# One hybrid SSD, gMLP and expert layer on one core: d_skip as rows, v and half of w_o in 512 columns, a shorter gelu

## The chip, the cores and the metric

The kernel runs on one core of a Trainium2 chip. The metric is the device time of one execution in microseconds (us). The engines are called PE (matmuls), DVE (VectorE), ACT (ScalarE), POOL (GpSimd) and SP, which here only issues loads. 16 DMA engines serve all queues of the core.

## What is computed

One layer of a backbone over 512 latent tokens and 256 context tokens with 1024 channels, cut to what the change touches:

```python
xm_l = rmsnorm(h, norm1_w) * (1 + sc1_l) + sh1_l      # sc, sh, g: slices of silu(c) @ ada_w + ada_b
p_l = xm_l @ w_in                                     # 512 x 7200
y_l, xh_l = ssd_scan_bidir(p_l[..., :N_SCAN], ...)    # conv, chunked scan in both directions
y = y + d_skip[:, None] * xh                          # 16 heads
g = rmsnorm_by_group(y * silu(z))                     # ssd branch
u, v = split(gelu(uv))                                # uv: 2048 columns of p_l
v = layernorm(v); sgu = u * (w_s mixes v over 128 positions + b_s)
merged = sigmoid(gate_a) * (ssd @ w_pa) + sigmoid(gate_b) * (sgu @ w_pb)
h = h + g1_l * (merged @ w_o)
h = h + g2_l * expert_choice_ffn(rmsnorm(h, norm2_w) * (1 + sc2_l) + sh2_l)   # 16 experts, 64 tokens each
return rmsnorm(h, final_norm_w)
```

## The kernel before

Everything is fp32. A product of two fp32 matrices is taken as three matmuls on halves: each operand is split into a high part (`wh`, a cast on ACT, L73) and a low part (`wl`, a subtraction on DVE, L74), and PE adds high × high, low × high and high × low in one accumulator. The helper `wsplit` does this for weights with high priority. Weight tiles of 1 MB come from a pool of two (`wtile`), loaded by SP.

The work in order of time. First SP loads x (L96, four loads) and the modulation weights `aw` (L193, two loads of 512 KB), then slices of `w_in` and the context tokens `ct` (L206). POOL issues small loads of its own in this time: the rows of the vectors (L88), `alog` (L124, one row of 32 numbers to all 128 partitions), `dtb` (L127) and the skip weights `dsk` (L130, two loads). PE begins with a matrix by vector product, `aux<-aw,scp` at L237, whose result is the first slice of the modulation; then it transposes the normalised x (L255) and the context (L261), and the first projection follows. The skip weights are read in the scan, at L527.

Then come convolution and scan by groups. v follows, through the helper `token_major` (L583): for each of four blocks of 256 columns and each half of the eight 128-row blocks of weights, 4 token tiles × 4 row blocks × 3 matmuls (L601 to L603), 96 instructions for a pair of halves. When a block's second half is through for a token tile, `evac` is called; for v it is `v_out`, which takes `gelu2` (L608 to L614: square on ACT, three DVE operations around a tanh on ACT) and after every second block the statistics for the layer norm (L623). While v runs, `steps(scans, 2)` puts pieces of the scan between its chunks. After the last block, L636 normalises v, and only then the tile that `w_s` is loaded into becomes free (L751); PE transposes `w_s` (L760) and mixes v. The u stage and the other projections use `cols` (L714 for the loads, L358 to L360 for the matmuls, 512 columns each); u calls `gelu2` as well, on 512 columns.

At the end of the mixer `token_major` runs again with `w_o` and `residual` (L915 to L921): multiply with the gate on DVE into the scratch `t0`, add x on DVE, square with a sum on ACT back into `t0`, which has one buffer. Between the chunks the router is prepared, and `logits(nb)` (L926 to L948) transposes finished columns and multiplies them with the router weights. Then come the choice of tokens, the eight pairs of experts with their weights in 1 MB pieces (L673, `fetch`), and the output.

The instructions are placed by a scheduler that follows the program order, priorities and free buffers, so the order on an engine changes with the code.

Of the kernel before, what the change touches and what calls it, by code (L numbers as in the profile page):

```python
# [20 lines left out]
NT = 4  # L21
# [12 lines left out]
def tile_backbone(  # L34
# [10 lines left out]
    def dram(t, off, ap):  # L45
        return bass.AP(tensor=t.tensor, offset=t.offset + off, ap=ap)

    def row_bc(t, off=0, n=1024):
        return dram(t, off, [[0, 128], [1, n]])
# [19 lines left out]
    def wtile():  # L69
        return wp.tile([128, 2048], F32, name="w")  # L70
# [5 lines left out]
    def wsplit(hi, lo, src, lo_eng=None):  # L76
        with tc.high_priority():
            split(hi, lo, src, lo_eng)
# [47 lines left out]
    G.memset(dtb, 0.0)  # L126
    nc.gpsimd.dma_start(dtb[0:32, :], dram(dt_bias, 0, [[1, 32], [1, 1]]))  # L127
    dsk = sp.tile([128, NK], F32, bufs=1)
    for s in range(2):
        nc.gpsimd.dma_start(dsk[64 * s:64 * s + 64, :], dram(d_skip, s, [[0, 64], [2, NK]]))  # L130

    def rsqrt(o, v, scr, n):

# [30 lines left out]
    def acc():  # L164
        return ps.tile([128, 512], F32, name="acc")
# [186 lines left out]
    def hl_tile(a, b):  # L352
        return [hl.tile([128, 1024], F32R, name=n)[:, :a * b].rearrange("p (a b) -> p a b", a=a) for n in ("wh", "wl")]
# [8 lines left out]
    def w_cols(src, c0, n):  # L362
        return dram(src, c0, [[src.shape[1], 128], [128 * src.shape[1], NK], [1, n]])
# [194 lines left out]
    def ahead(gen):  # L558

        cur = next(gen)  # L560
        for n in gen:
            yield cur
            cur = n
        yield cur
# [15 lines left out]
            scans = ssd_group(g)  # L580


    def token_major(src, n0, lh, ll, evac, wt=lambda nb: wtile()):  # L583

        def weights():
            for nb in range(4):
                w = wt(nb).rearrange("p (k n) -> p k n", k=NK)
                load(w, w_cols(src, n0 + 256 * nb, 256))
                for kh in range(2):
                    wh, wl = hl_tile(4, 256)  # L590
                    wsplit(wh, wl, w[:, 4 * kh:4 * kh + 4, :])
                    yield nb, kh, wh, wl

        for nb, kh, wh, wl in ahead(weights()):
            if kh == 0:
                pp = [acc()[:, :256] for _ in range(NT)]
            for t in range(NT):
                for k in range(4):
                    kt = 4 * kh + k
                    a = slice(128 * t, 128 * t + 128)  # L600
                    T.matmul(pp[t], lh[:, kt, a], wh[:, k, :], start=kt == 0, stop=False)  # L601
                    T.matmul(pp[t], ll[:, kt, a], wh[:, k, :], start=False, stop=False)  # L602
                    T.matmul(pp[t], lh[:, kt, a], wl[:, k, :], start=False, stop=kt == NK - 1)  # L603
                if kh == 1:
                    evac(nb, t, pp[t])
            yield

    def gelu2(o, p, a):  # L608

        S.activation(a, p, AF.Square)  # L610
        V.tensor_scalar(a, a, GELU_C * GELU_K, GELU_C, op0=OP.mult, op1=OP.add)
        V.tensor_mul(a, a, p)
        S.activation(o, a, AF.Tanh)
        V.scalar_tensor_tensor(o, o, 1.0, p, op0=OP.add, op1=OP.mult)  # L614

    vt = big.tile([128, NT, 1024], F32, name="F")
    bn = sp.tile([128, NT, 2, 6], F32, bufs=1)

    def v_out(nb, t, p):
        a = sp.tile([128, 512], F32, name="tm")[:, :256]  # L620
        gelu2(vt[:, t, 256 * nb:256 * nb + 256], p, a)
        if nb % 2:
            V.bn_stats(bn[:, t, nb // 2, :], vt[:, t, 256 * nb - 256:256 * nb + 256])  # L623

    for _ in token_major(W, 4128, xmh, xml, v_out):
        steps(scans, 2)
    steps(scans, 99)
    mv = sp.tile([128, NT, 2], F32, bufs=1)
# [51 lines left out]
    def fetch(n):  # L680
        while len(queue) < n:
            w = next(pieces, None)
            if w is None:
                return
            queue.append(w)
# [187 lines left out]
    def half(name, n=512):  # L873
        return rp.tile([128, 512], F32, name=name)[:, :n]
# [17 lines left out]
    def router_weights():  # L892

        p = aux()
        T.transpose(p[:, 0:32], mrow, ident[:32, :32])
        V.tensor_copy(mcol, p[:, 0:32])
        V.scalar_tensor_tensor(mcol[:, 8:16], mcol[:, 8:16], 1.0, mcol[:, 16:24], op0=OP.add, op1=OP.mult)
# [15 lines left out]
    h = big.tile([128, NT, 1024], F32, name="F")  # L913
    ssq = rp.tile([128, NT, 4], F32, bufs=1)

    def residual(nb, t, p):
        cs = slice(256 * nb, 256 * nb + 256)
        a = half("t0", 256)
        V.tensor_mul(a, p, g1b[:, cs])
        V.tensor_add(h[:, t, cs], a, x2[:, t, cs])  # L920
        S.activation(a, h[:, t, cs], AF.Square, accum_out=ssq[:, t, nb:nb + 1])  # L921

    pl, pt = aux(), aux()

    def logits(nb):

        at = full("m1").rearrange("p (k n) -> p k n", k=2)
        for k in (2 * nb, 2 * nb + 1):
            p = aux()
            for t in range(NT):  # L930
                T.transpose(p[:, 128 * t:128 * t + 128], h[:, t, 128 * k:128 * k + 128], ident)
            if k == NK - 1:
                V.tensor_copy(at[:, k % 2, :], p)
            else:
                S.copy(at[:, k % 2, :], p)
        for k in (2 * nb, 2 * nb + 1):
            if nb == 3:
                for t in range(NT):
                    T.matmul(pt[:, 16 * t:16 * t + 16], at[:, k % 2, 128 * t:128 * t + 128], rwl[:, k % 2, :],
                             start=False, stop=k == NK - 1, skip_group_check=True)  # L940
            else:
                g = slice(32 * (k % 4), 32 * (k % 4) + 32)
                T.matmul(pl[g, :], rw[:, k, :], at[:, k % 2, :], start=nb < 2, stop=k in (2, 3, 4, 5))
        if nb == 2:
            a = half("t0")
            S.copy(a, pl)
            for t in range(NT):
                T.matmul(pt[:, 16 * t:16 * t + 16], a[:, 128 * t:128 * t + 128], sel32[:, 0:16],  # L948
                         start=t == 0, stop=False, skip_group_check=True)

    for i, _ in enumerate(token_major(w_o.rearrange("l k n -> (l k) n"), 0, mgh, mgl, residual)):
        if i in {0:11}:
            fetch({0:11}[i])
        if i == 0:
            router_weights()
        elif i == 1:
            router_shift()
            V.tensor_copy(rwl, rw[:, 6:8, 0:16])
            before = half("t1").bitcast(BF)[:, :896]
            steps_ = half("t0").bitcast(I16)[:, :896]  # L960
            G.iota(steps_, pattern=[[1, 896]], base=-384, channel_multiplier=-1)
            V.tensor_scalar(before, steps_, 0.0, -2.0 ** -60, op0=OP.is_le, op1=OP.mult)
        elif i % 2 == 0:
            logits(i // 2 - 1)
    logits(3)
    es_xm.close()
    es_hl.close()
    es_mid.close()
# [160 lines left out]
    for pr in range(NE // 2):  # L1129
# [38 lines left out]
        def evac(name, c0, c1, pd):  # L1168
            a = half(name, c1 - c0)
            V.scalar_tensor_tensor(a, pd, gi[:, 0:1], g2k[:, c0:c1], op0=OP.mult, op1=OP.mult)  # L1170
            return a
# [99 lines left out]
```

## Time and profile before

| | us |
|---|---|
| median of the three times shown | 1179.45 |
| the other two | 1177.4 and 5647.97 (the first) |
| the profiled execution | 1177.17 |
| its span | 1175.4 |

The span runs from the first to the last instruction in the trace; 1.8 us of the profiled execution's time lie around it. Times in rows are counted from the start of the span. The stages, by the trace: loads and first modulation until about 26 us, first projection, convolution and scan until 237, v until 297.5, u and the other projections until 584, w_o until 646, routing until 661, the experts to the end. The mean granted clock of PE is 0.99 of 2.4 GHz.

### The profile page before, as it was taken

The numbers are of one execution on the slowest core, as the hardware profiler recorded it, in microseconds if no ns is written. First come the engines' busy times: TensorE is split into PE (matmuls) and PEld (weight loads), VectorE is DVE, ScalarE is ACT, GpSimd is POOL, SyncE is SP. The second block draws the span as 40 slices with busy tenths as digits, with TensorE's granted clock in tenths as the row PEclk, the third lists the DMA queues.
The fourth block names the chain that finished last, engine by engine and source line by source line (L and its number), as shares of the span: only waits on it lengthen the run. The fifth ranks groups of instructions, "written<-read, shape, count | busy, mean of one in ns | idle before, by whom it ended". The sixth has DMA issues, their size and how long they took to land.

```text
span 1175.4 us, 15016 instructions
## 1 busy us (share of the span) xinstructions
PE 1081.8 (92%) x5939; PEld 711.1 (61%) x5939; DVE 579.6 (49%) x1061; ACT 339.1 (29%) x645; POOL 66.4 (6%) x58
## 2 busy tenths in 40 slices
PE   2999899899999999999999699999898989899995
PEld 1778777799788888687897344343434343434333
DVE  2768999988797556536644711212030302121215
ACT  4343756553343223324333211010101010101002
POOL 2002232321000000100000000000000000000000
PEclk9999999999999999999999799999999999999998
DMA  9941624232576575525282898999999999999951
GB/s 213 248 121 54 200 90 161 73 108 73 179 219 210 191 241 186 173 74 177 72 326 97 298 374 314 395 406 393 407 393 409 393 408 396 405 397 402 402 182 72
DMA packets 149663, 291.85 MB, mean 248 GB/s; under 512 B 8468, under 2 KB 75188, under 8 KB 149592
## 3 DMA queue, kind: packets, MB, share of 16 engines
q1 hardware_dynamic: 149224, 290.79, 69.1%
q0 software_dynamic: 288, 0.07, 0.7%
q8 instruction: 47, 0.77, 0.3%
q14 instruction: 24, 0.20, 0.1%
q10 hardware_dynamic: 80, 0.02, 0.0%
HBM read 288.67 MB, written 2.18 MB: 247 GB/s over the span
## 4 chain that ended last, share of the span: by engine, by line
PE 78%; DVE 11%; ACT 4%; DMA 4%; issue 2%; POOL 0%; SPq 0%; DVEq 0%; ACTq 0%
PE x L1044 10%; PE pg L1044 10%; PE pu L1044 9%; PE pd L1044 8%; PE acc L358 7%; PE acc L360 7%; PE acc L359 7%; PE acc L603 2%; PE acc L601 2%; PE acc L602 2%; ACT m L1081 2%; DMA aw<-in_ada_w_dram 2%; PE pd L1164 1%; DVE gq L515 1%; DVE wl L74 1%
## 5 line engine op out<-in xcount | busy, mean ns | idle before, releaser
L358 PE MATMUL acc<-xmh,wh 128*128 128x512 f32 x352 | 139.1, 395 | 0.0
L359 PE MATMUL acc<-xml,wh 128*128 128x512 f32 x352 | 139.0, 395 | 0.0
L360 PE MATMUL acc<-xmh,wl 128*128 128x512 f32 x352 | 138.1, 392 | 0.0
L73 ACT CAST wh<-w 128x1024 fp32r<-128x1024 f32 (+1 forms) x84 | 84.4, 1005 | 170.5 <-PE acc L359 133.3
L74 DVE TENSOR_TENSOR wl<-w,wh 128x1024 fp32r<-128x1024 f32 (+1 forms) x81 | 95.8, 1183 | 68.2 <-ACT wh L73 67.2
L1170 DVE SCALAR_TENSOR_TENSOR t<-pd,gi,m 128x512 f32<-128x512 f32 (+2 forms) x17 | 12.2, 719 | 178.5 <-PE pd L1044 167.7
L1044 PE MATMUL x<-ot,F 128*128 128x128 f32 x512 | 74.9, 290 | 26.1 <-ACT m L1081 25.3
L1044 PEld LDWEIGHTS x<-ot,F 128*128 128x128 f32 x512 | 62.7, 193 | 44.1 <-ACT m L1081 36.6
L1125 DVE TENSOR_TENSOR F<-F,x 128x512 f32<-128x512 f32 x56 | 38.5, 688 | 91.2 <-PE x L1044 90.7
L1081 ACT ACTIVATE m<-x,mcol 128x128 f32<-128x128 f32 x64 | 29.3, 457 | 177.0 <-PE x L1044 177.0
L1044 PE MATMUL pg<-e,m 128*64 128x512 f32 x296 | 76.4, 602 | 0.0
L360 PEld LDWEIGHTS acc<-xmh,wl 128*128 128x128 f32 x352 | 66.3, 188 | 14.9 <-issue 1.2
L358 PEld LDWEIGHTS acc<-xmh,wh 128*128 128x128 f32 x352 | 66.3, 188 | 14.7 <-ACT wh L73 0.8
L601 PE MATMUL acc<-wh,xmh 128*128 128x256 f32 x256 | 73.5, 287 | 1.0 <-DVE F L614 1.0
L359 PEld LDWEIGHTS acc<-xml,wh 128*128 128x128 f32 x352 | 66.3, 188 | 13.1 <-issue 0.4
L603 PE MATMUL acc<-wl,xmh 128*128 128x256 f32 x256 | 73.3, 286 | 0.6 <-DVE wl L74 0.6
L1044 PE MATMUL pu<-e,m 128*64 128x512 f32 x304 | 73.7, 594 | 0.0
L602 PE MATMUL acc<-wh,xml 128*128 128x256 f32 x256 | 72.5, 283 | 0.0
L1044 PE MATMUL pd<-e,m 128*64 128x512 f32 x280 | 66.6, 594 | 0.0
L1144 DVE TENSOR_TENSOR t<-t,pu 128x512 f32<-128x512 f32 x16 | 10.3, 684 | 95.9 <-PE pu L1044 95.9
L358 PE MATMUL acc<-rh,wh 128*128 128x512 f32 x128 | 50.4, 396 | 0.8 <-ACT rh L73 0.5
L603 PEld LDWEIGHTS acc<-wl,xmh 128*128 128x128 f32 x256 | 49.0, 191 | 3.4 <-issue 2.5
(398 smaller groups left out, 1892.4 us busy)
## 6 DMA issues: line engine op xcount, KB each, us to landing
e<-in_w_up_dram SPq DMA_DIRECT2D x38, 1024.0 KB
e<-in_w_gate_dram SPq DMA_DIRECT2D x37, 1024.0 KB
e<-in_w_down_dram SPq DMA_DIRECT2D x35, 1024.0 KB
w<-in_w_in_dram SPq DMA_DIRECT2D x23, 1024.0 KB
f<-in_w_down_dram SPq DMA_DIRECT2D x20, 1024.0 KB
f<-in_w_up_dram SPq DMA_DIRECT2D x19, 1024.0 KB
f<-in_w_gate_dram SPq DMA_DIRECT2D x19, 1024.0 KB
e<-in_ada_w_dram SPq DMA_DIRECT2D x32, 512.0 KB
```

The costliest lines, as they stand in the source:

```text
L73: S.copy(hi, src)
L74: (lo_eng or V).tensor_sub(lo, src, hi.bitcast(F32))
L358: T.matmul(p, wh[:, kt, :], rh[:, kt, :], start=kt == 0, stop=False)
L359: T.matmul(p, wh[:, kt, :], rl[:, kt, :], start=False, stop=False)
L360: T.matmul(p, wl[:, kt, :], rh[:, kt, :], start=False, stop=kt == NK - 1)
L601: T.matmul(pp[t], lh[:, kt, a], wh[:, k, :], start=kt == 0, stop=False)
L602: T.matmul(pp[t], ll[:, kt, a], wh[:, k, :], start=False, stop=False)
L603: T.matmul(pp[t], lh[:, kt, a], wl[:, k, :], start=False, stop=kt == NK - 1)
L1044: return tc.keep_in_program_order(T.matmul(*a, **k))
L1081: S.activation(xt_[:, k, :], o, AF.Identity, scale=mcol[:, 8 + k:9 + k], bias=mcol[:, k:k + 1])
L1125: V.tensor_add(h[:, t, c0:c0 + 512], h[:, t, c0:c0 + 512], p)
L1170: V.scalar_tensor_tensor(a, pd, gi[:, 0:1], g2k[:, c0:c1], op0=OP.mult, op1=OP.mult)
```

## The change

Four things, in one diff. The skip weights come as one row of 16 numbers to all partitions (`dskr`), and two POOL copies pick the even and the odd heads for the two halves of the partitions. `token_major` takes a list of column cuts; v has two cuts of 512 columns, with weight tiles of 512 rows by 512 columns in the same 1 MB, and eight chunks as before; `v_out` takes 512 columns at once. w_o has one cut of 512 and two of 256; `residual` goes through a cut in pieces of 256, and the calls of `logits` follow the finished columns: two of them now come after the fifth chunk. `gelu2` takes the constants into a fused operation and into the scale of the tanh, one DVE operation less.

```diff
     dsk = sp.tile([128, NK], F32, bufs=1)
+    dskr = sp.tile([128, 2 * NK], F32, bufs=1)
+    nc.gpsimd.dma_start(dskr, row_bc(d_skip, 0, 2 * NK))
     for s in range(2):
-        nc.gpsimd.dma_start(dsk[64 * s:64 * s + 64, :], dram(d_skip, s, [[0, 64], [2, NK]]))
+        g = slice(64 * s, 64 * s + 64)
+        G.tensor_copy(dsk[g, :], dskr[g, :].rearrange("p (k s) -> p s k", s=2)[:, s, :])
...
-    def token_major(src, n0, lh, ll, evac, wt=lambda nb: wtile()):
+    def token_major(src, n0, lh, ll, evac, cuts):
...
-            for nb in range(4):
-                w = wt(nb).rearrange("p (k n) -> p k n", k=NK)
-                load(w, w_cols(src, n0 + 256 * nb, 256))
-                for kh in range(2):
-                    wh, wl = hl_tile(4, 256)
-                    wsplit(wh, wl, w[:, 4 * kh:4 * kh + 4, :])
-                    yield nb, kh, wh, wl
+            for c0, c1 in cuts:
+                n = c1 - c0
+                nk, half_ = 2048 // n, 1024 // n
+                for k0 in range(0, NK, half_):
+                    if k0 % nk == 0:
+                        w = wtile().rearrange("p (k n) -> p k n", k=nk)
+                        load(w, dram(src, n0 + c0 + 128 * k0 * src.shape[1],
+                                     [[src.shape[1], 128], [128 * src.shape[1], nk], [1, n]]))
+                    wh, wl = hl_tile(half_, n)
+                    wsplit(wh, wl, w[:, k0 % nk:k0 % nk + half_, :])
+                    yield c0, c1, k0, half_, wh, wl
...
         S.activation(a, p, AF.Square)
-        V.tensor_scalar(a, a, GELU_C * GELU_K, GELU_C, op0=OP.mult, op1=OP.add)
-        V.tensor_mul(a, a, p)
-        S.activation(o, a, AF.Tanh)
+        V.scalar_tensor_tensor(a, a, 1.0 / GELU_K, p, op0=OP.add, op1=OP.mult)
+        S.activation(o, a, AF.Tanh, scale=GELU_C * GELU_K)
         V.scalar_tensor_tensor(o, o, 1.0, p, op0=OP.add, op1=OP.mult)
...
-    def v_out(nb, t, p):
-        a = sp.tile([128, 512], F32, name="tm")[:, :256]
-        gelu2(vt[:, t, 256 * nb:256 * nb + 256], p, a)
-        if nb % 2:
-            V.bn_stats(bn[:, t, nb // 2, :], vt[:, t, 256 * nb - 256:256 * nb + 256])
+    def v_out(c0, c1, t, p):
+        gelu2(vt[:, t, c0:c1], p, sp.tile([128, 512], F32, name="tm"))
+        V.bn_stats(bn[:, t, c0 // 512, :], vt[:, t, c0:c1])
...
-    for _ in token_major(W, 4128, xmh, xml, v_out):
+    for _ in token_major(W, 4128, xmh, xml, v_out, ((0, 512), (512, 1024))):
...
-    def residual(nb, t, p):
-        cs = slice(256 * nb, 256 * nb + 256)
-        a = half("t0", 256)
-        V.tensor_mul(a, p, g1b[:, cs])
-        V.tensor_add(h[:, t, cs], a, x2[:, t, cs])
-        S.activation(a, h[:, t, cs], AF.Square, accum_out=ssq[:, t, nb:nb + 1])
+    def residual(c0, c1, t, p):
+        for c in range(c0, c1, 256):
+            nb, cs, ps_ = c // 256, slice(c, c + 256), slice(c - c0, c - c0 + 256)
+            a = half("t0", 256)
+            V.tensor_mul(a, p[:, ps_], g1b[:, cs])
+            V.tensor_add(h[:, t, cs], a, x2[:, t, cs])
+            S.activation(a, h[:, t, cs], AF.Square, accum_out=ssq[:, t, nb:nb + 1])
...
+    for i, end in enumerate(token_major(w_o.rearrange("l k n -> (l k) n"), 0, mgh, mgl, residual,
+                                        ((0, 512), (512, 768), (768, 1024)))):
```

POOL's queue at the start of the program before, from the constant `ones` to its first weight split; lines of the kernel before:

```order
13 L115 MEMSET ones 128x128
14 L117 IOTA jm 128x32
15 L124 DMA alog<-in_a_log_dram 128x32
16 L126 MEMSET dtb 128x1
17 L130 DMA dsk<-in_d_skip_dram 64x8x1
18 L127 DMA dtb<-in_dt_bias_dram 32x1
19 L130 DMA dsk<-in_d_skip_dram 64x8x1
20 L74 TENSOR_TENSOR wl<-w,wh 128x1024
```

And the same place in the changed kernel:

```order
13 L115 MEMSET ones 128x128
14 L117 IOTA jm 128x32
15 L124 DMA alog<-in_a_log_dram 128x32
16 L126 MEMSET dtb 128x1
17 L130 DMA dskr<-in_d_skip_dram 128x16
18 L127 DMA dtb<-in_dt_bias_dram 32x1
19 L133 COPY dsk<-dskr 64x8 x2
20 L74 TENSOR_TENSOR wl<-w,wh 128x1024
```

Two loads of 64 × 8 single elements have become one of 128 rows of 16, in the place of the first; the copies stand where the second load stood.

SP's queue where v ends and u begins, before: the last loads of v (L588), those of u (L714), then `w_s`, `b_s` and the first expert weights (L673):

```order
81 L588 DMA w<-in_w_in_dram 128x8x256
82 L714 DMA w<-in_w_in_dram 128x8x256 x3
83 L751 DMA e<-in_w_s_dram 128x8x128
84 L753 DMA e<-in_b_s_dram 128x1024
85 L673 DMA e<-in_w_gate_dram 128x2x1024 x2
```

And after, with the line numbers of the changed kernel (L596, L719, L756, L678):

```order
81 L596 DMA w<-in_w_in_dram 128x4x512
82 L719 DMA w<-in_w_in_dram 128x8x256 x4
83 L756 DMA e<-in_w_s_dram 128x8x128
84 L758 DMA e<-in_b_s_dram 128x1024
85 L678 DMA e<-in_w_gate_dram 128x2x1024 x2
```

One more weight load of the u stage stands ahead of `w_s`; on PE, 87 instead of 69 matmuls of that stage stand ahead of the transposes of `w_s`.

DVE in w_o before, around the end of the first cut (L919 and L920 are the two steps of `residual`, L74 the splits of weights; the rest prepares the router):

```order
699 L74 TENSOR_TENSOR wl<-w,wh 128x1024
700 L919 TENSOR_TENSOR t_5133<-acc,m_4986 128x256
701 L920 TENSOR_TENSOR F<-t_5133,F 128x256
702 L919 TENSOR_TENSOR t_5149<-acc,m_4986 128x256
703 L920 TENSOR_TENSOR F<-t_5149,F 128x256
704 L905 COPY t_5162<-aux 128x1
705 L908 COPY lshift<-aux 128x16
706 L962 TENSOR_SCALAR t_5169<-t_5170 128x896
707 L74 TENSOR_TENSOR wl<-w,wh 128x1024
```

And after (L925 and L926 are the steps of `residual` there):

```order
649 L74 TENSOR_TENSOR wl<-w,wh 128x1024
650 L925 TENSOR_TENSOR t_4887<-acc,m_4724 128x256
651 L926 TENSOR_TENSOR F<-t_4887,F 128x256
652 L925 TENSOR_TENSOR t_4891<-acc,m_4724 128x256
653 L926 TENSOR_TENSOR F<-t_4891,F 128x256
654 L925 TENSOR_TENSOR t_4901<-acc,m_4724 128x256
655 L926 TENSOR_TENSOR F<-t_4901,F 128x256
656 L74 TENSOR_TENSOR wl<-w,wh 128x1024
657 L925 TENSOR_TENSOR t_4905<-acc,m_4724 128x256
658 L926 TENSOR_TENSOR F<-t_4905,F 128x256
```

Before, the pieces of a cut come in fours, and preparations of the router lie between them; after, eight pieces of the first cut follow one another with one split among them, and behind these rows two pieces of the second cut come before the next split.

## Rows read from the trace of the kernel before

**Rows 1.** The page: busy time of PE, share of the span, instructions.

```profile
PE 1081.8 (92%) x5939; PEld 711.1 (61%) x5939; DVE 579.6 (49%) x1061; ACT 339.1 (29%) x645; POOL 66.4 (6%) x58
```

**Rows 2.** Waits of PE, whole span: us in total, times, longest.

```profile
PE aux L237 <- DMA aw<-in_ada_w_dram: 14.8, 1, 14.8
...
PE aux L760 <- DMA e<-in_w_s_dram: 1.6, 1, 1.6
PE acc L601 <- DVE F L614: 1.0, 1, 1.0
...
PE acc L603 <- DVE wl L74: 0.6, 1, 0.6
```

**Rows 3.** Critical chain, 0 to 30 us: start, us, what.

```profile
4.38 17.92 DMA aw<-in_ada_w_dram
...
25.92 4.16 PE aux L255 x19
```

**Rows 4.** DMA queues (packets, MB, share): 0:10; 8:10; 10:12; 14:16; 16:18; 0:22; 22:36.

```profile
q1 hardware_dynamic: 1653, 2.64, 76.3%
...
q0 software_dynamic: 59, 0.02, 45.8%
...
q0 software_dynamic: 15, 0.00, 113.2%
...
q0 software_dynamic: 16, 0.00, 176.6%
...
q0 software_dynamic: 2, 0.00, 31.2%
...
q1 hardware_dynamic: 3321, 4.16, 54.7%
...
q1 hardware_dynamic: 7017, 3.90, 99.9%
```

**Rows 5.** The tile `dsk`: its loads, and their time to landing.

```profile
L130 POOL DMA_DIRECT2D dsk<-in_d_skip_dram x2: 706/724/742, 5.0 to 6.5; - x2
...
DMA to landing us min/median/max: 9.3/12.5/15.6
```

**Rows 6.** The tile `alog`: time to landing of its load.

```profile
DMA to landing us min/median/max: 6.4/6.4/6.4
```

**Rows 7.** Timeline of ACT: the last normalisation of x.

```profile
12.17 2.19 ACT L226 ACTIVATE F<-F,rr 128x1024 f32<-128x1024 f32 x2 [2.02 <-DVE rr L143]
```

**Rows 8.** Timeline of PE in v (23 matmuls from first to second), in u (9).

```profile
291.04 0.28 PE L601 MATMUL acc<-wh,xmh 128*128 128x256 f32 x1
...
293.79 0.28 PE L603 MATMUL acc<-wl,xmh 128*128 128x256 f32 x1
...
340.82 0.40 PE L358 MATMUL acc<-xmh,wh 128*128 128x512 f32 x1
...
342.88 0.39 PE L358 MATMUL acc<-xmh,wh 128*128 128x512 f32 x1
```

**Rows 9.** Lines of DVE by form, 240 to 310 us: busy us, mean ns.

```profile
L612 DVE TENSOR_TENSOR tm<-tm,acc 128x256 f32<-128x256 f32 x16 | 6.6, 412 | 0.2
...
L611 DVE TENSOR_SCALAR tm<-tm 128x256 f32<-128x256 f32 x16 | 5.6, 351 | 0.2
L623 DVE BATCH_NORM_STATS2 bn<-F 128x6 f32<-128x512 f32 x8 | 5.5, 686 | 0.1
```

**Rows 10.** Timelines of DVE, SP and PE around the load of `w_s`.

```profile
307.06 2.98 DVE L636 TENSOR_SCALAR F<-F,mv,r 128x1024 f32<-128x1024 f32 x4
...
310.23 0.37 SPq L751 DMA_DIRECT2D e<-in_w_s_dram  x1
...
314.94 0.63 PE L760 MATMUL aux<-ident,e 128*128 128x128 f32 x4 [1.59 <-DMA e<-in_w_s_dram]
```

**Rows 11.** Timeline of DVE in w_o: two pieces of `residual` in a row.

```profile
607.21 0.42 DVE L919 TENSOR_TENSOR t<-acc,m 128x256 f32<-128x256 f32 x1 [1.88 <-PE acc L603]
...
608.73 0.42 DVE L919 TENSOR_TENSOR t<-acc,m 128x256 f32<-128x256 f32 x1 [0.64 <-ACT t L921]
```

More of the change, by code (lines that the diff above doesn't have):

```diff
@@ L580, in tile_backbone @@
             scans = ssd_group(g)
-    def token_major(src, n0, lh, ll, evac, wt=lambda nb: wtile()):
+    def token_major(src, n0, lh, ll, evac, cuts):
         def weights():
-            for nb in range(4):
-                w = wt(nb).rearrange("p (k n) -> p k n", k=NK)
-                load(w, w_cols(src, n0 + 256 * nb, 256))
-                for kh in range(2):
-                    wh, wl = hl_tile(4, 256)
-                    wsplit(wh, wl, w[:, 4 * kh:4 * kh + 4, :])
-                    yield nb, kh, wh, wl
-        for nb, kh, wh, wl in ahead(weights()):
-            if kh == 0:
-                pp = [acc()[:, :256] for _ in range(NT)]
+            for c0, c1 in cuts:
[9 more added lines that the diff above has]
+                    yield c0, c1, k0, half_, wh, wl
+        for c0, c1, k0, nk, wh, wl in ahead(weights()):
+            if k0 == 0:
+                pp = [acc()[:, :c1 - c0] for _ in range(NT)]
             for t in range(NT):
-                for k in range(4):
-                    kt = 4 * kh + k
+                for k in range(nk):
+                    kt = k0 + k
                     a = slice(128 * t, 128 * t + 128)
@@ L603, in token_major @@
                     T.matmul(pp[t], lh[:, kt, a], wl[:, k, :], start=False, stop=kt == NK - 1)
-                if kh == 1:
-                    evac(nb, t, pp[t])
-            yield
+                if k0 + nk == NK:
+                    evac(c0, c1, t, pp[t])
+            yield c1 if k0 + nk == NK else None
     def gelu2(o, p, a):
         S.activation(a, p, AF.Square)
-        V.tensor_scalar(a, a, GELU_C * GELU_K, GELU_C, op0=OP.mult, op1=OP.add)
-        V.tensor_mul(a, a, p)
-        S.activation(o, a, AF.Tanh)
+        V.scalar_tensor_tensor(a, a, 1.0 / GELU_K, p, op0=OP.add, op1=OP.mult)
+        S.activation(o, a, AF.Tanh, scale=GELU_C * GELU_K)
         V.scalar_tensor_tensor(o, o, 1.0, p, op0=OP.add, op1=OP.mult)
@@ L949, in logits @@
                          start=t == 0, stop=False, skip_group_check=True)
-    for i, _ in enumerate(token_major(w_o.rearrange("l k n -> (l k) n"), 0, mgh, mgl, residual)):
-        if i in {0:11}:
-            fetch({0:11}[i])
+    done = 0
+    for i, end in enumerate(token_major(w_o.rearrange("l k n -> (l k) n"), 0, mgh, mgl, residual,
+                                        ((0, 512), (512, 768), (768, 1024)))):
         if i == 0:
+            fetch(11)
             router_weights()
@@ L962, in tile_backbone @@
             V.tensor_scalar(before, steps_, 0.0, -2.0 ** -60, op0=OP.is_le, op1=OP.mult)
-        elif i % 2 == 0:
-            logits(i // 2 - 1)
-    logits(3)
+        elif i > 3:
+            while done < ready_:
+                logits(done)
+                done += 1
+        ready_ = end // 256 if end else done
+    while done < 4:
+        logits(done)
+        done += 1
     es_xm.close()
```

## The prediction

> **What bounds the kernel now.** I read five views: the page for the bound, the waits of the matrix engine (PE) for the places where it does not work, the critical chain of the first 30 us, the DMA queues over short stretches of that time, and timelines at the edited lines. On the page the reader is to see that PE is busy for 92% of the span [rows 1]. The edited stages v and w_o are PE work, so time is gained there only if PE works less or waits less. In the waits of PE, one row stands apart among the places that the change can reach: PE stands 14.8 us, once, for the DMA that brings `aw`, the first slice of the modulation weights [rows 2]. The others near the edits are small: 1.6 us for `w_s`, 1.0 and 0.6 us inside v.
>
> The chain says the same: `aw` is on it for 17.92 us, from 4.38 to 22.30; 3.62 us after that, at 25.92, L255 has begun, the transposes of x [rows 3]. `aw` is 1 MB. Why does it take 18 us? The queue rows answer that [rows 4]. By 10.0 us the hardware queue q1 had moved 2.64 MB. First in it stand x (four loads of 512 KB) and `aw` (two), 3.15 MB together, so 0.51 MB was missing. Then q1 nearly stops, while the software queue q0, POOL's, takes 113% of all 16 engines from 10 to 12 us with 15 packets that carry hardly a byte, and 177% from 14 to 16 with 16 packets (a share above 100% is a packet booked whole where it starts). That is 1.13 × 16 × 2 / 15 = 2.4 us and 1.77 × 16 × 2 / 16 = 3.5 us a packet; the two packets that start in 16 to 18 take 0.312 × 16 × 2 / 2 = 5.0 us each. These are the two loads of `dsk`: issued at 5.0 and 6.5, the slower one landed 15.6 us after its issue, near 22.1 us [rows 5], and `aw` landed at 22.3. I read it so that a packet of `dsk` sits on each of the 16 engines, and the last pieces of `aw` stand behind it.
>
> **The change part by part.** The sum is made against the profiled execution, 1177.17 us (span 1175.4); the median of the times shown is 1179.45, 2.3 above it.
>
> *d_skip.* Out go two loads whose pattern takes every second 4-byte element; in comes one load with a contiguous row of 64 bytes for each partition, and two small POOL copies. The nearest row for the new load is `alog`, the same kind with 128 bytes a partition, which landed in 6.4 us [rows 6] beside x at full load. In 8 to 10 us, before the long packets begin, q0 ran 59 packets for 45.8% of 16 engines, 0.458 × 16 × 2 / 59 = 0.25 us each at most [rows 4]. For 128 rows that is 8 × 0.25 = 2 us on each engine as the upper end, and nothing as the lower. Without `dsk` the missing 0.51 MB needs 0.51 / 0.28 = 1.8 us at the rate that q1 keeps when it has the engines to itself (3.90 MB in the 14 us from 22 to 36, at 99.9%); with 0.5 us for the row loads, `aw` is there at about 12.3, and PE starts L237 at 12.4, where it now starts at 22.4. What is late next? x must be normalised before L255: its last part ends on ACT at 14.36 [rows 7], and L255 now begins 3.62 us after `aw`, at 15.9, so it just holds. The context tokens and the next modulation slices are wanted 10 us earlier as well. By 36 us q1 has moved 4.16 + 3.90 = 8.1 MB in the kernel before; after, at the same point of PE's work, near 26 us, it can have moved 3.15 + 13.7 × 0.28 = 7.0. So the loads lose 1.1 MB, 3.8 us, of their lead. PE has no wait on these loads now, so I take off 0.5 us, and 3 us for the worst end. Value: 10.0 − 0.5 = 9.5 us, from 7 to 10.3. The two copies wait on POOL for the row; `dsk` is read only in the scan, far behind, so they cost nothing.
>
> The Trainium skill (DMA: Bandwidth & Descriptors, Rules for kernel authors) says that a last dimension that is not contiguous becomes one descriptor per element; the long packets here agree with that. Its Specifications say that under 512 bytes a transfer is not at line rate, which speaks against the 64-byte rows too; by `alog`, no run here shows them as costly as the elements.
>
> *v.* 384 matmuls of 256 columns become 192 of 512. From start to start, 23 of the narrow ones take 293.79 − 291.04 = 2.75 us, 0.1196 each, and 9 wide ones 342.88 − 340.82 = 2.06 us, 0.2289 each [rows 8] (the durations of 0.28 and 0.39 overlap). A pair against one wide: 0.2392 − 0.2289 = 0.0103 us, times 192 = 2.0 us. The Trainium skill (TensorE: Matmul & The Clock Gate, Back-to-back issue gap) gives a fixed 2.5 ns per matmul for isolated ones, which would be 0.5 us here; the trace shows four times that, and the trace decides.
>
> On DVE, gelu loses its tensor_scalar (16 × 351 ns), and the two other operations do the same elements in half as many instructions, each near the 0.69 us that the statistics take for 512 columns: 16 × (0.351 + 2 × 0.412) + 8 × 0.686 = 24.3 us now [rows 9], about 8 × 3 × 0.69 = 16.5 after. So the two PE waits in v on DVE, 1.0 and 0.6 [rows 2], go: v ends 2.0 + 1.6 = 3.6 us earlier on PE. They could stay if four wide evacuations at the end of a cut pile up; then it is 2.0.
>
> *u and w_s.* `w_s` may be loaded only when the normalisation of v, L636, is through (307.06 + 2.98 = 310.04); it is issued at 310.23, and PE starts its transposes at 314.94, 4.9 after L636, behind a wait of 1.59 [rows 10]. In the order of PE's instructions 69 matmuls of the u stage stand before these transposes now, and 87 after the change: 18 × 0.229 = 4.1 us more cover. v ends now at 314.94 − 1.59 − 69 × 0.229 = 297.5; so PE gets there at 297.5 − 3.6 + 87 × 0.229 = 313.8. L636 ends between 306.5 (DVE keeps up with v) and 310, and 4.9 later is 311.4 to 314.9: a wait of 0 to 1.1. So another 0.5 to 1.6 us goes. I take v and u together at 4.3 us, from 2 to 5.2.
>
> *w_o.* 96 pairs × 0.0103 = 1.0 us less on PE. Against this: `residual` still works in pieces of 256 columns through one scratch buffer, and a piece starts 1.52 us after the one before (608.73 − 607.21), 0.64 of it waiting for ACT to free `t0` [rows 11]. With 512 columns the first eight pieces all come at the end of the fourth chunk, 8 × 1.52 = 12.2 us in a row on DVE, and those of the next cut come after them. Behind them wait the weight splits of the last two chunks, and so PE. PE has chunks 5 and 6 (96 matmuls of 0.12 us, 11.5 us) and transposes of finished pieces to fill it: a new wait of 0 to 4 us. I take 1.5, near the lower end, since the fill nearly covers. Net: 0.5 us lost, from 1 gained to 3 lost.
>
> *After.* The expert stage has no wait for an expert weight among the waits of PE; it begins earlier and shifts. Sum: 1177.2 − 9.5 − 4.3 + 0.5 = 1163.9, so 1164 us. With all good ends 1160.7, with all bad ones 1171.2.
>
> **The rivals.** *A, `aw` is late anyway.* Its transfer in small pieces, not `dsk`, might hold it; PE then still starts at 22.4 and only 4.3 − 0.5 = 3.8 us go: 1173.4. For it speaks that 18 us is long even for a shared queue, and that nothing in the trace ties a packet to its load. Against it, that `dsk` and `aw` land within 0.3 us, and that q0 fills the engines while q1 stops.
>
> *B, w_o piles up.* If PE finds nothing to do while the first eight pieces go through, w_o loses 12.2 − 1.0 = 11.2: 1177.2 − 9.5 − 4.3 + 11.2 = 1174.6. For it: a single scratch buffer. Against: PE has two chunks to work on in other accumulators.
>
> *C, slower: rows to all partitions cost like the elements.* The new load has 128 rows, 8 for each engine. The 18 packets that start from 14 to 18 us take 56.5 + 10.0 = 66.5 us, 3.7 us each; at that price an engine is held 8 × 3.7 = 29.6 us, `aw` lands near 12 + 29.6 = 41.6, 19.3 later than before: 1177.2 + 19.3 − 3.8 = 1192.7. The start breaks even at (22.3 − 12.0) / 8 = 1.3 us a row, and the whole kernel at (10.3 + 3.8) / 8 = 1.8. Against it: 0.25 us at most for a row of `alog`.
>
> *D, more than I see.* DVE is relieved in u too, by 0.4 us for each of 8 gelus. Were all of it, and the 4.1 us moved ahead of `w_s`, PE time, another 3.2 + 4.1 = 7.3 us would give 1157; but PE has no other wait there to lose.
>
> **How the numbers follow.** My forecast has 0.80, A 0.08, B 0.05, C 0.03, D 0.04. The forecast's own range is 1160.7 to 1171.2; A and B lie above, so the range goes to 1174, and to 1157 on the other side for D. A measurement of this kernel tells about 2% from no change, 23.5 us, so below some 1155 or above some 1201: faster takes D and the far end of the forecast, 0.06; slower is C, 0.03; the same, 0.91.
>
> **What would show it.** In the profile after, PE's wait for `aw` is near 5 us and it begins near 12.4; q0 never takes more than half of the engines between 10 and 18 us. PE's starts in v are 0.229 apart, its waits in v on DVE are under 0.5, the wait for `w_s` is under 1.2. In w_o PE waits 0 to 4 us. The expert stage keeps its length. I am wrong if PE still begins after 15 us, if the context or a modulation slice becomes the wait that replaces `aw`, or if w_o's wait passes 4 us.

## The result, and the profile after

The changed kernel takes 1164.78 us (median; 1160.99 to 1167.52), the kernel before 1178.43 beside it (1175.02, 1177.4, 1179.45 and a first execution of 5647.97, which the ratio leaves out): a ratio of 0.989, 95% interval 0.985 to 0.993. The forecast was 1164 in a range of 1157 to 1174, and no change by the 2% that were set. The profiled execution took 1164.31 us with a span of 1162.5, 12.9 less than before.

Where the 12.9 us lie is read from the starts of the same lines of code in both traces:

| point on PE (the gate: DVE) | before | after | gained up to there |
|---|---|---|---|
| first modulation matmul | 22.44 | 12.95 | 9.5 |
| first matmul of v | 236.9 | 227.3 | 9.6 |
| last gate of the projections (`ga` times accumulator) | 584.7 | 570.4 | 14.3 |
| first of the last logits | 643.7 | 628.1 | 15.6 |
| transposes of the affinities, behind the router | 656.6 | 641.0 | 15.6 |
| second pass of expert weights | 667.43 | 654.26 | 13.2 |
| end of the span | 1175.4 | 1162.5 | 12.9 |

So the start gave 9.5 us, v and u 4.7, w_o 1.3, and 2.4 were given back in the first expert matmuls, a place that the prediction had called a mere shift. Up to the last gate the granted clock does not distort the comparison: both traces have one dip of the same size there (0.83 in 105 to 115 us before, 0.83 in 95 to 105 after), and 1.0 elsewhere.

The waits of PE after, the answer to [rows 2] (us in total, times, longest):

```profile
PE aux L240 <- DMA aw<-in_ada_w_dram: 5.2, 1, 5.2
...
PE aux L743 <- DVE e L740: 2.4, 1, 2.4
...
PE aux L765 <- DMA e<-in_w_s_dram: 1.0, 1, 1.0
...
PE aux L937 <- DVE F L926: 0.7, 1, 0.7
PE aux L945 <- ACT m L941: 0.6, 1, 0.6
```

The wait for `aw` fell from 14.8 to 5.2, the two waits inside v are gone, the one for `w_s` is 1.0, and in w_o no wait is new: the lines of L937 and L945 waited 0.7 and 0.6 before as well (L931 and L939 there). The row of L743, a sum for a later slice of the modulation, had 1.7 before (L738). The critical chain of the start, against [rows 3], shows `aw` for 8.39 us in place of 17.92:

```profile
4.43 8.39 DMA aw<-in_ada_w_dram
...
16.44 5.19 PE aux L258 x24
```

The DMA queues from 8 to 10 us, then from 10 to 12, against [rows 4] (packets, MB, share of 16 engines):

```profile
q0 software_dynamic: 67, 0.02, 59.9%
q1 hardware_dynamic: 515, 0.26, 43.4%
...
q1 hardware_dynamic: 1345, 0.68, 112.6%
q0 software_dynamic: 63, 0.01, 2.6%
```

Where q0 held 113% of the engines, it now holds 2.6%, and q1 moves 0.68 MB in 2 us, `aw` among it. But from 8 to 10 us, before the stretch that I had named, q0 takes more than half of the engines, and q1 moves 0.26 MB there. That is mostly not the row of d_skip: without it (b_elems_late below) q0 has 57.9% in these 2 us and q1 moves 0.29 MB, and with the row of `alog` gone as well (a_rows_late) it is 1.4% and 0.68 MB. The row load of d_skip landed after 6.8 us, near the 6.4 of `alog` in [rows 6]:

```profile
DMA to landing us min/median/max: 6.8/6.8/6.8
```

In v the wide matmuls start 0.2267 us apart (21 of them between these two rows of PE's timeline), and DVE has 24 wide instructions where it had 56 narrower ones [rows 8, 9]. First PE, then DVE by lines (busy us, mean ns):

```profile
275.73 0.39 PE L609 MATMUL acc<-wh,xmh 128*128 128x512 f32 x1
...
280.49 0.39 PE L609 MATMUL acc<-wh,xmh 128*128 128x512 f32 x1
```

```profile
L621 DVE SCALAR_TENSOR_TENSOR F<-F,acc 128x512 f32<-128x512 f32 x8 | 5.4, 681 | 0.8 <-ACT F L620 0.7
L619 DVE SCALAR_TENSOR_TENSOR tm<-tm,acc 128x512 f32<-128x512 f32 x8 | 5.4, 680 | 1.7 <-ACT tm L618 1.7
L628 DVE BATCH_NORM_STATS2 bn<-F 128x6 f32<-128x512 f32 x8 | 5.3, 684 | 0.0
```

That is 16.1 us (16.5 were forecast). The issue of `w_s` stands at 298.23, 12.0 us earlier than in [rows 10]:

```profile
298.23 0.37 SPq L756 DMA_DIRECT2D e<-in_w_s_dram  x1
```

What was given back shows in the granted clock of PE, in tens of us behind w_o. Columns: stretch, its length, PE busy (matmuls), granted clock, DMA share, GB/s. Before, then after:

```profile
640.00:650.00 10.00, 5.41 (x40) 0.79 0.78 280
650.00:660.00 10.00, 3.73 (x18) 0.53 1.05 393
660.00:670.00 10.00, 9.45 (x52) 1.00 0.46 153
```

```profile
620.00:630.00 10.00, 8.70 (x69) 0.95 0.33 101
630.00:640.00 10.00, 2.81 (x12) 0.50 1.03 403
640.00:650.00 10.00, 8.45 (x30) 0.53 0.49 181
650.00:660.00 10.00, 8.90 (x52) 1.00 0.66 218
```

In both, the clock goes from 2.4 to 1.2 GHz after PE's two waits of 0.7 and 0.6 us at the last transposes and logits: near 645.8 before, as the wait for the router begins, and near 629 after, in the last logits. By the shares of these stretches it stays low for 4.2 + 9.4 = 13.6 us before and 1 + 10 + 9.4 = 20.4 after. It is back 2.8 us after the transposes of the affinities have begun before, and only 8.4 us after them in the changed kernel. So the first 3 us of the first pass of expert weights ran at half the clock:

```profile
641.00 1.01 PE L1037 MATMUL pd<-ident,aff 128*16 128x128 f32 x4 [5.72 <-DVE t L1019]
...
646.33 5.20 PE L1056 MATMUL pg<-e,m 128*64 128x512 f32 x16
...
654.26 3.65 PE L1056 MATMUL pg<-e,m 128*64 128x512 f32 x16
```

5.20 us for the first pass, 3.65 for the second; before, both take 3.65. No line of this code was changed.

### The profile page after: what moved, and what is told of

Its sections match the earlier page's. It is cut to its first block, busy times and chain, and to the rows that moved or that the text cites. A ratio compares the mean times of both kernels' runs of the same rounds, so it can differ in the third digit from the quotient of the medians.

```text
span 1162.5 us, 14364 instructions
## 1 busy us (share of the span) xinstructions
PE 1080.3 (93%) x5651; PEld 696.8 (60%) x5651; DVE 569.2 (49%) x1021; ACT 335.7 (29%) x629; POOL 66.5 (6%) x59
## 4 chain that ended last, share of the span: by engine, by line
PE 80%; DVE 10%; ACT 4%; DMA 3%; issue 2%; POOL 0%; SPq 0%; DVEq 0%; ACTq 0%
PE pg L1056 10%; PE x L1056 10%; PE pu L1056 10%; PE pd L1056 8%; PE acc L361 8%; PE acc L363 7%; PE acc L362 7%; PE acc L611 2%; PE acc L610 2%; PE acc L609 2%; ACT m L1093 2%; PE pd L1176 1%; DVE seg L516 1%; PE aux L537 1%; DVE gq L518 1%
## 5 line engine op out<-in xcount | busy, mean ns | idle before, releaser
L74 DVE TENSOR_TENSOR wl<-w,wh 128x1024 fp32r<-128x1024 f32 (+1 forms) x81 | 96.0, 1186 | 71.4 <-ACT wh L73 70.9
L1056 PE MATMUL x<-ot,F 128*128 128x128 f32 x512 | 75.9, 292 | 26.1 <-ACT m L1093 25.3
L362 PEld LDWEIGHTS acc<-xml,wh 128*128 128x128 f32 x352 | 66.3, 188 | 12.9
L1156 DVE TENSOR_TENSOR t<-t,pu 128x512 f32<-128x512 f32 x16 | 10.3, 683 | 95.9 <-PE pu L1056 95.9
L609 PE MATMUL acc<-wh,xmh 128*128 128x512 f32 (+1 forms) x160 | 56.5, 354 | 0.0
L611 PE MATMUL acc<-wl,xmh 128*128 128x512 f32 (+1 forms) x160 | 56.1, 351 | 0.1
L610 PE MATMUL acc<-wh,xml 128*128 128x512 f32 (+1 forms) x160 | 56.1, 351 | 0.0
L362 PE MATMUL acc<-rl,wh 128*128 128x512 f32 x128 | 50.2, 393 | 0.0
```

Of the source, the lines that this page charges most:

```text
L74: (lo_eng or V).tensor_sub(lo, src, hi.bitcast(F32))
L362: T.matmul(p, wh[:, kt, :], rl[:, kt, :], start=False, stop=False)
L1056: return tc.keep_in_program_order(T.matmul(*a, **k))
```

## The experiments

Theory S: packets of the element loads stood on all DMA engines ahead of `aw`. Theory C, formed after the result: the granted clock behind the router takes back part of the gain. Times are medians beside the kernel before on the same chip; where a kernel ran once, that is said.

**b_rows: the start alone.**

```diff
+    nc.gpsimd.dma_start(dskr, row_bc(d_skip, 0, 2 * NK))
     for s in range(2):
-        nc.gpsimd.dma_start(dsk[64 * s:64 * s + 64, :], dram(d_skip, s, [[0, 64], [2, NK]]))
+        g = slice(64 * s, 64 * s + 64)
+        G.tensor_copy(dsk[g, :], dskr[g, :].rearrange("p (k s) -> p s k", s=2)[:, s, :])
```

> The kernel before with one part of the change: d_skip as one row to all partitions. Theory S (the packets of the element loads stand on all 16 engines ahead of the last pieces of aw): PE begins its first modulation matmul near 12.9 us in place of 22.4, and v begins 9.5 us earlier, as in the changed kernel; the whole is 1177 - 9.5 = about 1168 us, with 3 us to either side from the clock of PE behind the router. Rival A (aw is late by itself, and something else in the change freed it): PE still begins near 22 us and the time is that of before.

Measured 1169.62 against 1175.77, ratio 0.994 (0.992 to 0.997). PE begins as S says:

```profile
12.77 1.94 PE L240 MATMUL aux<-aw,scp 128*32 128x256 f32 x16 [5.15 <-DMA aw<-in_ada_w_dram]
```

v begins at 227.3, 9.6 us earlier. A falls: nothing but the skip loads was changed. At the end only 5.9 of the 9.6 us are left in the profile, span 1169.5. The clock was low once more than in the kernel before, at 460 us, and behind the router for 3.8 + 10 + 6.6 = 20.4 us in place of 13.6:

```profile
460.00:470.00 10.00, 8.02 (x34) 0.83 0.71 223
630.00:640.00 10.00, 7.35 (x51) 0.81 0.56 207
640.00:650.00 10.00, 3.42 (x15) 0.50 1.04 397
650.00:660.00 10.00, 9.40 (x39) 0.67 0.27 84
```

**b_elems_late: the same element loads, later.**

```diff
+    V.tensor_copy(dsk, dth[:, 0:NK])
+    for s in range(2):
+        nc.gpsimd.dma_start(dsk[64 * s:64 * s + 64, :], dram(d_skip, s, [[0, 64], [2, NK]]))
```

These lines stand behind the first dt; the two loads at the start are taken out.

> The kernel before with its two element loads of d_skip unchanged, but made to wait for the first dt values, near 70 to 80 us by the new count. Theory S: the price of these loads is their place, not their number; PE begins near 12 us, a little earlier than with the row load, and near 75 us only one weight load of 1 MB with over 15 us to spare is held up: about 1168 us, like the row load. Rival R (the loads cost what they cost wherever they stand): the 9 us come back as a wait of PE behind 75 us, and the time stays near 1177.

Measured 1169.27, 0.995 (0.993 to 0.997), the same as the row load. The loads landed in 8.4 to 10.7 us even there, but PE waits for nothing of theirs:

```profile
DMA to landing us min/median/max: 8.4/9.5/10.7
```

R falls: it is their place beside `aw` that cost 9 us. This run also shows what the prediction could only infer, that the long packets are those of `dsk`: from 70 to 100 us POOL issues no other load, and q0 (packets, MB, share of 16 engines) has

```profile
q0 software_dynamic: 64, 0.00, 21.5%
```

That is 0.215 × 16 × 30 / 64 = 1.6 us a packet on average; from 82 to 84 us, with no packet of q1 beside them, 12 of them take 131.5% of the engines, 3.5 us each.

PE began at 13.68, not near 12: `alog` and the vectors stood there still, and a row load less brought nothing. Kernels with the same loads at the start as the changed one begin between 12.77 (b_rows) and 13.94 (a_longgelu), so half a microsecond there is no difference. Behind the router the clock of this run lay as in the kernel before, although v begins 10.3 us earlier (226.6 against 236.9), and the first pass of expert weights took 3.65 us:

```profile
630.00:640.00 10.00, 5.42 (x38) 0.79 0.82 313
640.00:650.00 10.00, 3.73 (x20) 0.53 0.99 370
650.00:660.00 10.00, 9.45 (x53) 1.00 0.47 165
```

Its span, 1164.8, keeps 10.6 us: 8.8 from the start and the rest up to v, since its clock did not dip near 105 us. So the earlier start does not by itself make the low stretch longer.

**b_elems_twice: the loads doubled.**

```diff
+    dsk2 = sp.tile([128, NK], F32, bufs=1)
+    for s in range(2):
+        nc.gpsimd.dma_start(dsk2[64 * s:64 * s + 64, :], dram(d_skip, s, [[0, 64], [2, NK]]))
```

> The kernel before with both element loads issued a second time into a tile that nothing reads. Theory S, by the 2.4 to 5.0 us of a packet and 16 packets for each load: PE begins 6 to 9 us later than 22.4, at 28 to 31 us, if the second pair still comes ahead of the last pieces of aw; at least the context tokens come so much later. Rival A: PE begins at 22.4 us as before.

Measured 1189.92 in one run, 14 us slower than before. PE began at 20.9, so the second pair, issued from 8.0 us on, came behind `aw`; it held what follows:

```profile
PE aux L240 <- DMA aw<-in_ada_w_dram: 13.3, 1, 13.3
...
PE aux L258 <- DVE mod L247: 7.3, 1, 7.3
```

L247 is a small addition on DVE, and its input was there at 24.4 us. It came at 34.01: ahead of it in DVE's queue stood the split of the first weights, which waited for ACT's cast of the same weights, which waited for their load. Timelines of ACT and of DVE:

```profile
32.62 0.62 ACT L73 CAST wh<-w 128x512 fp32r<-128x512 f32 x1 [18.32 <-DMA w<-in_w_in_dram]
...
33.27 0.69 DVE L74 TENSOR_TENSOR wl<-w,wh 128x512 fp32r<-128x512 f32 x1 [9.95 <-ACT wh L73]
...
34.01 0.27 DVE L247 TENSOR_SCALAR mod<-aux,adc,vc 128x2 f32<-128x2 f32 x1
```

The expected start of 28 to 31 was wrong, the weaker form of S right: the transposes of the context begin at 39.93, 7.0 us later than before. At the start of v the second pair had cost 10.8 us (247.7 against 236.9), a little more than the first. At the end the spans are 12.7 us apart (1188.1 against 1175.4), some 3 of them from behind the router, where the clock was low for longer than before.

**a_rows5: the price of a row load.**

```diff
+    dskx = sp.tile([128, 4, 2 * NK], F32, bufs=1)
+    for s in range(4):
+        nc.gpsimd.dma_start(dskx[:, s, :], row_bc(d_skip, 0, 2 * NK))
```

> The changed kernel with four more loads of the d_skip row to all partitions, into a tile that nothing reads, ahead of the copies. It measures the price of a row load beside x and aw. If a row costs 0.25 to 0.3 us on its engine, 8 rows for each engine and load give 2.0 to 2.4 us, and PE begins 8 to 10 us later, near 21 to 23. If rows cost a tenth of that, PE begins under 1 us later than 12.95.

Measured 1167.11 in one run. PE began 0.3 us later than after the change, but its transposes were broken by a wait, and those of the context began at 26.21 in place of 22.83:

```profile
13.26 1.93 PE L243 MATMUL aux<-aw,scp 128*32 128x256 f32 x16 [5.46 <-DMA aw<-in_ada_w_dram]
...
20.66 4.94 PE L261 MATMUL aux<-ident,F 128*128 128x128 f32 x20 [1.26 <-DVE mod L250]
```

v begins 3.4 us later too (230.7 against 227.3). Four loads for 3.4 us, 0.85 each, under half of the 2 us that I held for the upper end; from 12 to 18 us q0 takes 99.4, 50.7 and 23.2% of the engines in steps of 2 us, which is 3.5 us of all 16. PE's start, by which the expectation was put, could not show this price: the four were issued between 6.8 and 9.7 us, and most of their packets' time lies behind 12 us, when `aw` was nearly through. Rival C is far off.

**a_v256 and a_longgelu: v and gelu, one undone at a time.**

```diff
-    for _ in token_major(W, 4128, xmh, xml, v_out, ((0, 512), (512, 1024))):
+    for _ in token_major(W, 4128, xmh, xml, v_out, ((0, 256), (256, 512), (512, 768), (768, 1024))):
```

with the statistics after every second cut, and, in the other kernel,

```diff
-        V.scalar_tensor_tensor(a, a, 1.0 / GELU_K, p, op0=OP.add, op1=OP.mult)
-        S.activation(o, a, AF.Tanh, scale=GELU_C * GELU_K)
+        V.tensor_scalar(a, a, GELU_C * GELU_K, GELU_C, op0=OP.mult, op1=OP.add)
+        V.tensor_mul(a, a, p)
+        S.activation(o, a, AF.Tanh)
```

> The changed kernel with v in four cuts of 256 columns again, all else kept, the short gelu too. Points of the changed kernel: v begins at 227.3 us, the last gate of the projections on DVE (L866) starts at 570.4. Theory P (the pitch of the matmuls is v's gain): that point comes 2.0 us later, 192 x 0.0103. Theory D (DVE's relief is the gain, and most of it is the wide operations): 3 to 4 us later, with PE waits on DVE inside v. Rival: nothing, if the load of w_s sets the end of v and u anyway.

> The changed kernel with the old gelu, one tensor_scalar more in v and u, 16 on DVE with 512 columns, 0.42 us each. Theory P: under 0.5 us later at the last L866, since PE hides it. Theory D: DVE is what v and u wait for; 1.5 to 3.4 us later, as a longer wait for w_s or waits on DVE.

Measured 1165.33 and 1167.61, one run each, too close to the runs of the changed kernel to compare whole times. The expected points (L866) are no measure either: dips of the clock near 105 and 465 us move them by up to 2 us between kernels with the same code there. v's own length is clean. Its first and last row in the changed kernel, with narrow v, and with the long gelu (starts, first to last):

```profile
L611 PE MATMUL acc<-wl,xmh x64: 388/389/585, 227.9 to 283.0; 128*128 128x512 f32 x64
```

```profile
L611 PE MATMUL acc<-wl,xmh x128: 278/283/470, 226.0 to 285.4; 128*128 128x256 f32 x128
```

```profile
L611 PE MATMUL acc<-wl,xmh x64: 387/389/581, 227.1 to 283.3; 128*128 128x512 f32 x64
```

55.1 us, 59.4 and 56.2; other kernels with the same v as the changed one have 55.0 to 55.5. b_rows, with both undone, has 60.2 on its first line, where the changed kernel has 55.2 (227.3 to 282.5):

```profile
L604 PE MATMUL acc<-wh,xmh x128: 278/283/466, 227.3 to 287.5; 128*128 128x256 f32 x128
```

So 512 columns are worth 4.3 us of v with the short gelu and about 4 with the long one, near D's figure. The pitch is 192 × (0.2392 − 0.2267) = 2.4 of them, a wait of PE for DVE 0.9 (L529, for `seg`); where the last microsecond lies was not traced. The gelu is worth about 1, between P and D, against a scatter of 0.5.

**a_wo256 and a_wo512: w_o.**

```diff
-                                        ((0, 512), (512, 768), (768, 1024)))):
+                                        ((0, 256), (256, 512), (512, 768), (768, 1024)))):
```

with the logits at their old places, and in the other kernel

```diff
-                                        ((0, 512), (512, 768), (768, 1024)))):
+                                        ((0, 512), (512, 1024)))):
```

> The changed kernel with w_o in four cuts of 256 columns and the calls of logits where they stood before. From the last L866 to the first of the last logits (L945) the changed kernel takes 628.1 - 570.4 = 57.7 us. By the pitch alone it is 1.0 us longer, 58.7, as in the kernel before (59.0). By the prediction's step, in which the eight pieces of the first cut cost PE 1.5 us, it is 0.5 us shorter, 57.2.

> The changed kernel with the whole of w_o in two cuts of 512 columns. By the pitch alone another 96 x 0.0103 = 1.0 us less from the last gate to the first of the last logits, 56.7 in place of 57.7. By the chain through the one scratch buffer, eight pieces of 1.52 us stand behind the last matmul instead of four: four of them more after PE's end, 4 to 6 us longer, 61 to 63, and the logits wait for them. I expect the second.

From the last gate to the last logits: 631.3 − 572.3 = 59.0 us with four narrow cuts, 57.7 with the change, 633.2 − 569.0 = 64.2 with two wide ones (whole runs 1167.38 and 1169.68). So the first wide cut is worth 1.3 us and stops nothing, and a second one loses 6.5, more than the 4 to 6 expected: the eight pieces of the last cut still start 1.52 us apart, 0.64 of it for ACT to free the one scratch buffer, PE's transposes wait for them, and the clock is at 0.5 from 624 us on, ahead of the logits. The waits of PE in w_o with two wide cuts:

```profile
PE aux L937 <- DVE F L926: 5.1, 2, 2.6
```

**a_warm and a_warm2: PE kept at work behind w_o.** `keep(n)` adds n matmuls of 256 columns into a bank whose content is dead; nothing reads them.

```diff
+    def keep(n):
+        for _ in range(n):
+            tc.keep_in_program_order(T.matmul(pl[:, 0:256], ident, h[:, 0, 0:256], start=True, stop=True))
...
     rows_ = [acc() for _ in range(2)]
+    keep(7)
...
+    keep(12)
```

with `keep(1)` twice in the last logits; in a_warm 3, 3, 10 and 25. The transposes and matmuls of the router around them are held in program order as well.

> The changed kernel with 41 matmuls of 256 columns on PE whose result nothing reads, put in the waits behind w_o and the router: 3 and 3 around the last transposes, 10 before L1013 and 25 behind it. Theory C (the granted clock falls to 0.5 there and stays low into the first expert weights, 628.5 to 649.2 us in the changed kernel, which gave back 2.6 us of the gain): the clock stays at 1.0, the first expert matmuls take 3.65 us in place of 5.20, the transposes ahead of them 1.16 in place of 2.08, and 3 to 5 us go: 1160 us, with less spread. Rival: the clock falls as before, the added matmuls run at the lower level, delay L1013 and the rest by 1 to 3 us, and the time is 1165 to 1168.

Measured 1167.69, 0.992 (0.989 to 0.995). The clock was 1.00 in every stretch from 626 to 658 us, so the first half of C held; but one added matmul takes 0.44 us (10.96 us for 25, which are 50 instructions in the trace), so they were too long, and the affinities came at 648.10 in place of 641.00:

```profile
637.08 10.96 PE L933 MATMUL aux<-F,ident 128*128 128x256 f32 x50
648.10 0.60 PE L1049 MATMUL pd<-ident,aff 128*16 128x128 f32 x4
...
657.61 3.65 PE L1068 MATMUL pg<-e,m 128*64 128x512 f32 x16
```

From there to the second pass it took 657.61 − 648.10 = 9.5 us, 13.3 in the changed kernel.

> The changed kernel with fewer added matmuls than the first trial, whose clock held at 1.0 but whose 41 took 0.437 us each, 18 us, and pushed the rest 7 us back: now 1 and 1 around the last transposes, 7 before L1013, 12 behind it, 9.2 us in all inside waits of 0.7, 0.6, 3.3 and 5.7 us. Theory C: the clock stays at 1.0 behind w_o; from the transposes of the affinities to the second pass of expert weights it takes 9.5 us, as in the first trial, in place of 13.3; with 0.9 each for the logits and L1013, less up to 0.9 where the added ones run over, the time falls by 4 to 5 us: 1160 us, and the runs lie closer together than 1161 to 1167.5. Rival: with gaps left between them the clock falls after all, and the time stays at 1165 or rises.

Measured 1159.42 (1158.24 to 1159.69), 0.984 (0.983 to 0.986) of the kernel before: as expected, with runs closer together than those of the changed kernel.

```profile
639.64 0.60 PE L1049 MATMUL pd<-ident,aff 128*16 128x128 f32 x4 [0.95 <-DVE t L1031]
...
643.13 3.65 PE L1068 MATMUL pg<-e,m 128*64 128x512 f32 x16
...
649.51 3.65 PE L1068 MATMUL pg<-e,m 128*64 128x512 f32 x16
```

The first pass takes 3.65 us, and 9.9 lie between the affinities and the second. C is shown: PE's clock, and not the change, had taken back the 2.4 us. From the first of the last logits to the second pass it takes 23.6 us here and 26.2 in the changed kernel; with the router as it was and nothing added it takes 23.7 before and 23.8 in b_elems_late, where the clock was low for 13.6 us, and 26.1 in b_rows, where it was low for 20.4. So the added matmuls are worth about 2.5 us where the low stretch is long, and nothing where it is short. The other 2.2 of the 4.7 us between the spans of 1157.8 and 1162.5 are there already at the last gate (568.2 against 570.4), in code that the edit does not touch: the clock of this execution did not dip near 100 us. That all four runs of a_warm2 are fast is more than the 2.5 us explain, and why was not traced. The granted clock still fell for a short while (0.88 in 620 to 630, 0.95 in the next ten), before the experts begin.

**a_rows_late and a_best: the row loads behind the context.**

```diff
+        load(alog, row_bc(a_log, 0, 32))
+        load(dskr, row_bc(d_skip, 0, 2 * NK))
```

behind the loads of `ct` on SP; both are gone from POOL. a_best adds the `keep` of a_warm2.

> The changed kernel with the row loads of alog and d_skip issued by SP behind the context tokens, no longer beside x and aw. If the two cost q1 about 1.2 us between 8 and 10 us (0.26 MB there in place of 0.50), PE begins near 11.8 us in place of 12.95. Rival: aw's own 3.15 MB with x set 12.5 us, and PE begins over 12.5. If alog is late for the exponential that stands before the context's squares on ACT, PE waits instead at the context's transposes and nothing is won at L291.

> Both of the other two: the row loads behind the context tokens, and PE kept at work behind w_o. If both hold, 1160 - 1 = about 1159 us; if the row loads bring nothing, as a_warm2.

a_rows_late took 1159.74 in one run. PE began where expected, now behind the normalisation of x (L139) and no longer behind `aw`, and the gain held at L291 (23.64 against 24.69):

```profile
11.90 1.94 PE L240 MATMUL aux<-aw,scp 128*32 128x256 f32 x16 [4.34 <-DVE sc L139]
```

The 5 us by which this one run lies under the changed kernel are not all from there: its clock did not dip near 100 us, and behind the router it was low for 17 us in place of 20.4. a_best took 1160.23 (1157.57 to 1162.3), 0.985 (0.983 to 0.987): not better than a_warm2, though PE began at 11.67, where a_warm2 began at 13.27. The profile is of its slowest run. Its clock dipped at two places where that of a_warm2 did not, and at the last gate it is 2.9 us behind (571.1 against 568.2):

```profile
100.00:110.00 10.00, 9.14 (x48) 0.91 0.46 137
...
460.00:470.00 10.00, 10.00 (x38) 0.83 0.63 202
```

So a_warm2 is the version whose runs all lie below those of the changed kernel (1158.24 to 1159.69 against 1160.99 to 1167.52, in separate sets of runs; the ratios to the kernel before, 0.983 to 0.986 and 0.985 to 0.993, still touch); whether the late row loads add to it stays open.

## Why the prediction was right, point by point

- **d_skip**: 9.5 us forecast, 9.5 measured, and b_rows, b_elems_late and b_elems_twice show the mechanism. Two sizes inside were off, and that they cancel is luck: `aw` came 0.5 us later than I said (12.82, not 12.3), and the loss of lead that I priced at 0.5 us took nothing that is left at the start of v (9.6 gained); it shows only as a wait of 0.3 at the context's transposes. What made `aw` later stays open: 0.5 us is within what the start varies by, b_elems_late has 13.55 without the row of d_skip, and `alog`, which I took as the measure of a cheap row, holds the engines from 8 to 10 us.
- **v**: 3.6 forecast; v is 60.2 − 55.2 = 5.0 us shorter. The end of both waits (1.6) is as said; the pitch gave 2.4 and not 2.0, since I had taken that of the wide matmuls from u (0.2289; in v it is 0.2267). The last microsecond was not in the sum.
- **u and w_s**: the wait for `w_s` fell from 1.6 to 1.0, in the range of 0 to 1.1. With v, 4.7 us came where 4.3 were forecast; PE's wait at the sums of a modulation slice, L743, grew from 1.7 to 2.4 us, which I had not seen.
- **w_o**: a wrong step. "A new wait of 0 to 4 us; I take 1.5": there was none. The two chunks and the transposes covered the eight pieces wholly, as the waits show, and w_o gained 1.3 where I had a loss of 0.5. By the pitch of 0.2267 the 96 pairs are worth 1.2 of it. The pile-up that I feared is real, but one cut later (a_wo512).
- **After**: "it begins earlier and shifts" left out 2.4 us. The rows of the clock before were there to be read (0.79 and 0.53 behind w_o); I did not ask how far they vary. That the start is earlier is not the reason: b_elems_late reaches v as early and gave nothing back, b_rows gave back 2.3. What decides between 13.6 and 20.4 us at the lower clock is not shown here.

The errors of w_o (1.8 us too dear) and of the experts (2.4 too cheap) nearly cancel, so that the sum is closer than its terms; this too is luck. A, B and C did not happen. The range was said to take in A and B, but B at 1174.6 lay above its end of 1174.

## What to carry to other kernels

Look at a software queue's share against its bytes: a small load of single elements that fills the DMA engines while it moves nothing belongs behind the loads that the first matmul waits for, or is replaced by rows. A wider matmul is worth its pitch and, where the evacuating engine is near its limit, what its fewer instructions free; a chain through one scratch buffer is hidden only while another cut's matmuls stand behind it. Where an engine waits some microseconds, read the granted clock of the stretch behind: idle time that costs nothing by itself can make the next matmuls run at half speed, and added matmuls inside the wait gave back 2.5 us here, where the clock had been low for long. Two executions of one stage at different clocks differ by as much as a change is worth: read the clock of both before a difference is put down to the code.

## What I had not expected of the hardware

- A packet of the element loads takes 2.4 to 5.0 us on its engine beside other traffic (by the shares in [rows 4]) and is slow when nothing else runs: 12 of them took 3.5 us each in b_elems_late, where the loads landed in 8.4 to 10.7 us.
- A load of one row to 128 partitions is not free either: about 0.85 us each for the four of a_rows5, behind `aw`.
- The same waits of PE end in different clocks: near 105 us the clock was 0.83 in b_rows and 1.00 in b_elems_late, with the same 1.7 us wait ahead. From the first modulation matmul to the start of v that makes 214.5 against 212.9 us. It can be part of the 6.5 us that lie between the runs of the changed kernel, of which only one has a trace: the fastest, 1160.99, has the highest mean clock, 0.991, but the other three, 3.2 us apart, have 0.986, 0.987 and 0.986.
